# Second RWKV layer of a four-layer encoder: the first half of the key product by split parts, with a new table of rank offsets

## The chip, the cores and the metric

The kernel runs on one core of a Trainium2 chip. The metric is the device time of one execution in microseconds, as the median of several runs. TensorE (PE) multiplies matrices, VectorE (DVE) and ScalarE (ACT) work on tiles in the on-chip memory, GpSimd (POOL) does little here, and SyncE (SP) issues the DMAs.

## What is computed

Four layers with residual adds on an input of 256 tokens by 1024 channels in float32. Each layer is a token mixer and a SwiGLU FFN of 2816 inner channels, both behind an RMS norm. The mixers are, in order: RWKV-7 time mixing, stick-breaking attention, sparse attention over selected keys, and RWKV-7 again. The change is in the last of these. Of its reference only this bears on it:

```
shifted = jnp.pad(h, ((0, 0), (1, 0), (0, 0)))[:, :-1]
xm = h[:, :, None, :] + (shifted - h)[:, :, None, :] * mix
rkv = jnp.einsum('bsjd,jde->bsje', xm[:, :, :3], w_rkv)
r, k, v = rkv[:, :, 0], rkv[:, :, 1], rkv[:, :, 2]
...
kk = heads(k * k_k)
```

So the key `k` is a 1024 by 1024 product of the mixed input. From it, the decay and the gates come the factors of a recurrence over the tokens, which is computed in four chunks of 64 tokens for 16 heads.

## The kernel before

Activations lie with channels on the 128 partitions and the 256 tokens along the free axis, in eight channel blocks. Weights come from the DRAM in 401 pieces of 128 x 1024 float32 (`raw`, four buffers). There are two ways to multiply with such a piece:

- Unsplit: `raw_piece` hands the float32 piece to PE. PE's trace shows one such source matmul as two records.
- Split: `piece` copies the piece to the rounded type float32r (`wh`, a CAST, on ACT or DVE) and subtracts that from the piece on DVE (`wl`). The input is split in the same way (`split`: a cast for the high part, a subtraction on DVE for the low part). `mm3` then adds three products: `wh` by the high input, `wh` by the low input, `wl` by the high input. `wh` and `wl` have three buffers each.

`SPLITS` says for each of the two RWKV layers which products are split. A letter `k` splits the whole key product, and `K` its second half only. The key product has two halves of 512 output channels. The first half (key pieces `ka`, accumulated in two banks named `kp`) goes through the eight channel blocks in turn, as its inputs come from the norm; the second half (`gemm2`) follows from the stored split inputs `kx`. With `K`, the mixed input of a channel is written to `xk` in full, used there by the first half, and also split to `kx` for the second. With `k`, it is written to a small rotating tile `xm` and split to `kx`, which both halves use. The lines that choose:

```
sk, sk2, sv_ = [n in SPLITS[j] for n in "kKv"]
...
w = [v3(t, 2) for t in (piece(key) if sk else (raw_piece(key),))]
if sk:
    split(kx[:, 0, c], kx[:, 1, c], xm("mk", c))
else:
    mix(xk[:, c, :], "mk", c)
    if sk2:
        split(kx[:, 0, c], kx[:, 1, c], xk[:, c])
```

The order of the work around it: the FFN of the third layer ends with its down product (`dn`), whose last sum is added to `xt`. The squares (`sq`) are summed over the channels by PE (`ss`) and make the scale `rstd` (`rstdm`, `rstda`). DVE then forms the normed input and its difference to the previous token, both in `pre`, and the mixed inputs. PE meanwhile multiplies `lora_in`, which needs only `xt`. Behind the keys come the receptance `rp` (from `prx`), the gate `g`, the small products `lw` and `la` (64 rows of the array), `sc` (kept in `SB`), and the values `vp`. DVE copies 32x32 blocks of `SB` together (`blocks`), inverts them in 31 steps (`xtmp`, `inv`), copies the result to `XT` and transposes it (`xd`). The products `cmb` and then the recurrence (`xu`, `qu`, `pS`, `Y` on 64x64 parts of the array) follow, and the output product `po`.

The order within each engine isn't the order of the code. A planner (class `Plan`) records all operations, estimates a cost for each, ranks them by the longest path behind them, and schedules them by list over the engines. It chooses among engines where an operation can run on more than one (casts and copies on ACT or DVE), gives out the buffers, and puts in two filler matmuls at a time (`warm_o`) where PE would have too little to do in a stretch of time. It repeats this for 16 rounds, and then once more from its best with the table `NUDGES`: each entry (seed, first, last, width) draws random offsets for the ranks of a range of operations. The schedule with the shortest planned time is emitted.

Of the kernel before, what the change touches and what calls it, by code (L numbers as in the profile page):

```python
# [189 lines left out]
class Queue:  # L190
# [91 lines left out]

WAIT = {"tensor": 85.0, "vector": 55.0, "scalar": 40.0, "gpsimd": 40.0, "sync": 0.0}

SPLITS = ('K', 'K')
FREE = ("raw", "xm")

BIAS = {"vector": 2.0}
# [1753 lines left out]
```

## Time and profile before

| what | value |
|---|---|
| median of 3 runs | 1381.39 us (1380.25 to 1381.43) |
| the profiled execution's own time | 1380.69 us |
| its span, first to last instruction | 1378.9 us |
| fp32 `kp<-xk` matmul records, both RWKV layers | 128, of which 64 in the second |
| split `kp<-kx` matmul records, both layers | 192, of which 96 in the second |
| second RWKV layer, from the last down matmuls to the output product | about 1001 to 1190 us of the span |

Times in the profile are in microseconds from the span's start, means of one instruction in ns. A row of the timeline has start, length, engine, line, operation, out<-in, the shapes, and in brackets the idle time in front of it with what ended it. Rows with xN are N like instructions in a row; their lengths overlap, since an instruction's end is seen later than the next one's start. All operations have the line of the planner's call (L785), so the names of the tiles tell them apart.

### The profile page before, as it was taken

The page shows a single profiled execution, that of the slowest core. Times are in us where ns is not written, and L with a number is a line of the kernel's source. Part 1 is how long each engine was busy: PE and PEld are TensorE (multiplying, and loading weights), DVE is VectorE, ACT ScalarE, POOL GpSimd, SP SyncE. Part 2 cuts the span into 40 slices and gives each one's busy share as a digit, 9 for nine tenths or more (in the row PEclk, how much of TensorE's full clock was granted, in tenths as well). Part 3 has the DMA queues.
Part 4 walks back from the last instruction along what each step waited for, and adds up shares of the span by engine and source line. Part 5 has one row for each costly group of instructions (what it writes and reads, how often), then busy time and mean ns, then how long its engine had stood idle before and what let it go on. Part 6 is the DMA issues. An engine that isn't in the chain of part 4 may idle for free.

```text
span 1378.9 us, 25431 instructions
## 1 busy us (share of the span) xinstructions
PE 1368.9 (99%) x10134; PEld 1189.6 (86%) x10134; DVE 1123.5 (81%) x1981; ACT 765.2 (55%) x1285; POOL 7.5 (1%) x16
## 2 busy tenths in 40 slices
PE   9999999999999999999999999999999999999998
PEld 7988898888888898888887798888888888988887
DVE  7899688896676789886589888986589996899864
ACT  4866665454456755454456875444357466655432
POOL 0000000000000000000000000000000000000000
PEclk9999999999999999999999999999999999999999
DMA  5533155566654355555554445555534231556563
GB/s 188 171 106 109 39 177 184 183 198 188 198 169 154 108 153 190 193 185 193 189 183 154 160 133 189 189 194 187 195 93 141 93 95 47 169 187 195 185 209 112
DMA packets 61333, 220.04 MB, mean 160 GB/s; under 512 B 6816, under 2 KB 8352, under 8 KB 60960
## 3 DMA queue, kind: packets, MB, share of 16 engines
q1 hardware_dynamic: 61216, 218.44, 49.1%
q8 instruction: 79, 1.29, 0.4%
q14 instruction: 38, 0.31, 0.1%
HBM read 217.36 MB, written 1.05 MB: 158 GB/s over the span
## 4 chain that ended last, share of the span: by engine, by line
PE 94%; DVE 4%; ACT 1%; issue 0%; DMA 0%; SPq 0%; ACTq 0%; DVEq 0%
PE dn L785 18%; PE gate L785 18%; PE up L785 18%; PE po L785 7%; PE kp L785 4%; PE rp L785 3%; PE qk L785 3%; PE vps L785 3%; PE vp L785 2%; PE z L785 2%; PE q L785 2%; PE k L785 2%; PE sc L785 1%; PE lora_in L785 1%; PE Y L785 1%; PE attn_o L785 1%
## 5 line engine op out<-in xcount | busy, mean ns | idle before, releaser
L785 ACT CAST wh<-raw 128x1024 fp32r<-128x1024 f32 x339 | 354.7, 1051 | 356.5 <-PE dn L785 114.8
L785 DVE TENSOR_TENSOR wl<-raw,wh 128x1024 fp32r<-128x1024 f32 x375 | 453.2, 1220 | 75.9 <-ACT wh L785 69.6
L785 PE MATMUL up<-xg,wh 128*128 128x512 f32 x704 | 253.9, 395 | 0.0
L785 PE MATMUL gate<-xg,wh 128*128 128x512 f32 x704 | 253.4, 395 | 0.0
L785 PE MATMUL dn<-h,wh 128*128 128x512 f32 x720 | 247.3, 391 | 0.0
L785 PE MATMUL dn<-h,wl 128*128 128x256 f32 x704 | 197.3, 280 | 0.0
L785 PE MATMUL up<-xg,wl 128*128 128x256 f32 x704 | 196.9, 280 | 0.0
L785 PE MATMUL gate<-xg,wl 128*128 128x256 f32 x704 | 196.9, 280 | 0.0
L785 PEld LDWEIGHTS dn<-h,wh 128*128 128x128 f32 x720 | 134.2, 188 | 30.6
L785 PEld LDWEIGHTS gate<-xg,wh 128*128 128x128 f32 x704 | 132.0, 188 | 30.6
L785 PEld LDWEIGHTS up<-xg,wh 128*128 128x128 f32 x704 | 131.9, 187 | 30.5
L785 PEld LDWEIGHTS up<-xg,wl 128*128 128x128 f32 x704 | 132.9, 189 | 0.1
L785 PEld LDWEIGHTS gate<-xg,wl 128*128 128x128 f32 x704 | 132.9, 189 | 0.1
L785 PEld LDWEIGHTS dn<-h,wl 128*128 128x128 f32 x704 | 132.9, 189 | 0.0
L785 DVE TENSOR_TENSOR xt<-xt,dn 128x256 f32<-128x256 f32 x64 | 26.7, 418 | 42.4 <-PE dn L785 41.7
L785 DVE TENSOR_TENSOR gus<-gus,rstd 128x512 f32<-128x512 f32 x88 | 59.8, 685 | 1.1
L785 PE MATMUL vp<-xv,raw 128*128 128x256 f32 x256 | 57.7, 382 | 0.1
L785 PEld LDWEIGHTS vp<-xv,raw 128*128 128x128 f32 x256 | 47.8, 190 | 7.6 <-issue 0.7
L785 PE MATMUL rp<-prx,wh 128*128 128x256 f32 x256 | 50.1, 295 | 0.0
L785 PE MATMUL po<-yhl,wh 128*128 128x256 f32 x256 | 48.9, 291 | 0.1
L785 PE MATMUL po<-ohl,wh 128*128 128x256 f32 x256 | 48.3, 289 | 0.0
L785 PE MATMUL qk<-xg,wh 128*128 128x512 f32 x128 | 46.3, 403 | 0.0
(326 smaller groups left out, 2380.4 us busy)
## 6 DMA issues: line engine op xcount, KB each, us to landing
raw<-in_wts_dram SPq DMA_DIRECT2D x401, 512.0 KB, 3.6
lora<-in_lora_dram SPq DMA_DIRECT2D x2, 1280.0 KB, 9.6
xt<-in_xT_dram SPq DMA_DIRECT2D x4, 256.0 KB, 4.0
lora<-in_lora_dram SPq DMA_DIRECT2D x2, 512.0 KB, 5.3
inv<-in_id_dram SPq DMA_DIRECT2D x2, 512.0 KB, 4.6
out_dram<-xt SPq DMA_DIRECT2D x8, 128.0 KB, 1.9
sbt<-in_consts_dram SPq DMA_DIRECT2D x1, 512.0 KB, 4.2
consts<-in_consts_dram SPq DMA_DIRECT2D x1, 288.0 KB, 3.8
```

The costliest lines, as they stand in the source:

```text
L785: getattr(getattr(nc, o.eng), method)(*map(real, args), **{k: real(a) for k, a in kw.items()})
```

## The change

`SPLITS` gives the second RWKV layer `k` in place of `K`: its first half of the keys is multiplied by split parts of weights and inputs too, and `xk` falls away there. The first RWKV layer keeps `K`. The table `NUDGES` has other entries (219 for 221), which moves instructions in all layers.

```
-    (903826, 3056, 3356, 3000), (539854, 3023, 3143, 8000), (863608, 3279, 3287, 8000), (659967, 3402, 3452, 3000),
...
+    (258298, 3255, 3305, 300), (585931, 3338, 3458, 1000), (427633, 4293, 4593, 1000), (808878, 5009, 5029, 3000),
...
-SPLITS = ('K', 'K')
+SPLITS = ('K', 'k')
```

The whole program has 32 float32 key matmuls less (of the source), 96 split ones more, four casts to `wh` and four subtractions to `wl` more, and 12 filler matmuls more. Three places show how the order moves. The line of the planner's call is L784 in the changed kernel, since the table is a line shorter.

PE, from the end of the third layer's down product to the first key products of the second RWKV layer, before:

```order
L785 MATMUL dn<-h,wh_10335 128x256 x2
L785 MATMUL dn<-h,wl_10343 128x256
L785 MATMUL ss<-sq,ones 128x256
L785 MATMUL lora_in<-xt_69,lora 128x256 x4
L785 MATMUL ss<-sq,ones 128x256
L785 MATMUL lora_in<-xt_72,lora 128x256 x4
L785 MATMUL lora_in<-xt_73,lora 128x256 x4
L785 MATMUL lora_in<-xt_74,lora 128x256 x4
L785 MATMUL kp<-xk,raw_10282 128x256 x4
```

The same place in the changed kernel:

```order
L784 MATMUL dn<-h,wl_10343 128x256
L784 MATMUL ss<-sq,ones 128x256 x3
L784 MATMUL lora_in<-xt_69,lora 128x256 x2
L784 MATMUL ss<-sq,ones 128x256
L784 MATMUL lora_in<-xt_69,lora 128x256 x2
L784 MATMUL lora_in<-xt_72,lora 128x256 x4
L784 MATMUL lora_in<-xt_73,lora 128x256 x4
L784 MATMUL lora_in<-xt_74,lora 128x256 x4
L784 MATMUL kp<-kx,wh_10358 128x256 x2
L784 MATMUL kp<-kx,wl_10371 128x256
```

Two `ss` products that stood among the down products stand behind them now, and the first key products are split triples with the pieces 10358/10371.

DVE, from the last subtractions for the down product to the scale of the norm, before:

```order
L785 TENSOR_TENSOR wl_10320<-raw_10256,wh_10312 128x1024
L785 TENSOR_TENSOR wl_10343<-raw_10269,wh_10335 128x1024
L785 MEMSET pre 128x8
L785 TENSOR_TENSOR xt_74<-xt_74,dn 128x256 x4
L785 TENSOR_SCALAR rstdm<-ss 128x256
```

The same place in the changed kernel, where 10371, 10393 and 10421 are the first three key pieces:

```order
L784 TENSOR_TENSOR wl_10343<-raw_10261,wh_10333 128x1024
L784 TENSOR_TENSOR xt_74<-xt_74,dn 128x256 x2
L784 MEMSET pre 128x8
L784 TENSOR_TENSOR wl_10371<-raw_10285,wh_10358 128x1024
L784 TENSOR_TENSOR wl_10393<-raw_10321,wh_10385 128x1024
L784 TENSOR_TENSOR xt_74<-xt_74,dn 128x256 x2
L784 TENSOR_TENSOR wl_10421<-raw_10335,wh_10412 128x1024
L784 TENSOR_SCALAR rstdm<-ss 128x256
```

Two subtractions of key pieces stand between the adds of the last two channel blocks, and a third between the last adds and `rstdm`. The fourth key piece is subtracted later, among the key inputs:

```order
L784 SCALAR_TENSOR_TENSOR xm<-pre,vecs 128x256
L784 TENSOR_TENSOR wl_10551<-raw_10354,wh_10509 128x1024
L784 TENSOR_TENSOR kx<-xm,kx 128x256
L784 SCALAR_TENSOR_TENSOR pre<-xt_74,vecs,rstd 128x256
L784 TENSOR_TENSOR wl_10576<-raw_10381,wh_10547 128x1024
```

The first of these subtractions is for the key piece of channels 6 and 7; the second already belongs to the second half of the keys.

PE, ahead of the recurrence of the second RWKV layer, before (each filler has a row for its weights and one for its product):

```order
L785 MATMUL cmb_11863<-XT,zs 32x32 x16
L785 MATMUL xu<-QC,XT 64x64 x4
L1879 LDWEIGHTS warm_x
L1879 MATMUL warm_o<-warm_x 128x256
L1879 LDWEIGHTS warm_x
L1879 MATMUL warm_o<-warm_x 128x256
L785 MATMUL cmb_11893<-xd,SB 32x32 x16
```

and in the changed kernel:

```order
L784 MATMUL cmb_11899<-xd,SB 32x32 x16
L784 MATMUL bn<-prhl,bonesr 128x512 x2
L1878 LDWEIGHTS warm_x
L1878 MATMUL warm_o<-warm_x 128x256
L1878 LDWEIGHTS warm_x
L1878 MATMUL warm_o<-warm_x 128x256
L784 MATMUL cmb_11931<-XT,zs 32x32 x16
L1878 LDWEIGHTS warm_x
```

Before, gate products (`pg`) stood between the first `cmb` products and the fillers came behind the first `xu`, six of them up to the second `xu`; now the gate products are all ahead of `cmb`, and fourteen fillers stand between the first `cmb` and the second `xu`, the last row shown being the first of the next six.

109 rows, old and new, of the table NUDGES are left out of this document.

## Prediction

> **What bounds the kernel now.** I read the page first, then the windows over the second recurrent layer, then the timelines of TensorE (PE) and VectorE (DVE) in it.
>
> ```profile
> span 1378.9 us, 25431 instructions
> PE 1368.9 (99%) x10134; PEld 1189.6 (86%) x10134; DVE 1123.5 (81%) x1981; ACT 765.2 (55%) x1285; POOL 7.5 (1%) x16
> PE 94%; DVE 4%; ACT 1%; issue 0%; DMA 0%; SPq 0%; ACTq 0%; DVEq 0%
> ```
>
> PE is busy for all but 10 us and carries 94% of the chain that ended last. That is the mean of the whole kernel; the changed layer has to be read by itself. The windows (us; then busy time and count of PE, weight loads, DVE, ACT, POOL; PE clock; DMA) run from the last matmuls of the FFN before the layer to its output product:
>
> ```profile
> 1001.00:1011.00 10.00, 10.00 (x53) 8.94 (x53) 5.03 (x13) 3.81 (x7) 0.00 (x0) 1.00 0.01 2
> 1011.00:1048.00 37.00, 37.00 (x256) 33.75 (x255) 36.99 (x70) 28.06 (x53) 0.36 (x1) 1.00 0.50 157
> 1048.00:1063.00 15.00, 15.00 (x116) 12.80 (x115) 14.72 (x27) 12.66 (x24) 0.00 (x0) 1.00 0.43 120
> 1063.00:1083.00 20.00, 20.00 (x213) 17.87 (x211) 19.51 (x34) 8.90 (x16) 1.86 (x2) 1.00 0.24 76
> 1083.00:1100.00 17.00, 16.86 (x95) 13.73 (x96) 16.25 (x39) 5.66 (x12) 0.00 (x0) 1.00 0.35 113
> 1100.00:1137.00 37.00, 35.61 (x589) 30.52 (x587) 35.95 (x76) 25.12 (x48) 0.00 (x0) 1.00 0.28 92
> 1137.00:1175.00 38.00, 37.47 (x714) 31.23 (x711) 24.06 (x65) 23.91 (x65) 0.00 (x0) 1.00 0.15 48
> ```
>
> Here two engines are full at once. From 1011 to 1137 us DVE is busy for 95 to 100% of every window, as PE is; only behind 1137, in the recurrence proper, does DVE fall to 24.06 of 38 us. Which of the two is followed shows at the end of that stretch:
>
> ```profile
> 1129.33 1.28 PE L785 MATMUL cmb<-xd,SB 32*32 32x32 f32 x64 [0.73 <-DVE xd L785]
> 1136.12 0.61 PE L1879 MATMUL warm_o<-warm_x 128*128 128x256 bf16 x4
> 1138.15 0.25 DVE L785 TENSOR_SCALAR Sd<-Sn,dc 128x64 f32<-128x64 f32 x1 [0.52 <-ACT Sn L785]
> ```
>
> PE stood idle for 0.73 us until DVE had transposed the inverted blocks (`xd`); DVE's own first wait comes at 1138.15. So **DVE's work sets when the recurrence starts**, and PE is only just not late for it.
>
> **The change part by part.** The key product of the first half loses its unsplit form. One unsplit source matmul is two records of 128x256; a split one is three, two with `wh` and one with `wl`.
>
> ```profile
> 1010.74 10.52 PE L785 MATMUL kp<-xk,raw 128*128 128x256 f32 x48
> ...
> 1029.93 0.40 PE L785 MATMUL kp<-kx,wh 128*128 128x256 f32 x2
> 1030.17 0.28 PE L785 MATMUL kp<-kx,wl 128*128 128x256 f32 x1
> 1030.29 0.40 PE L785 MATMUL kp<-kx,wh 128*128 128x256 f32 x2
> ```
>
> 48 records in 10.52 us, the last of which lasts about 0.38, make (10.52 - 0.38)/47 = 0.216 us each, 0.432 a source matmul. A split triple repeats after 1030.29 - 1029.93 = 0.36 us, all three together. There are 32 (8 channels, 4 column blocks): 32 x (0.432 - 0.360) = **2.3 us less on PE**. [...] The row shows 0.360, so the sum uses that.
>
> What it costs: four weight pieces now need a cast (ACT) and a subtraction (DVE).
>
> ```profile
> L785 DVE TENSOR_TENSOR wl<-raw,wh 128x1024 fp32r<-128x1024 f32 x16 | 19.3, 1214 | 0.6 <-PE po L785 0.6
> L785 ACT CAST wh<-raw 128x1024 fp32r<-128x1024 f32 x12 | 12.5, 1042 | 2.5 <-DMA raw<-in_wts_dram 2.4
> ```
>
> Four casts are 4.2 us of ACT, busy 28.06 of 37 us in the tightest window; I cost them at nothing (bounds 0 and 1.0, one cast late). Four subtractions are 4.9 us of DVE, and here the order of the instructions decides. DVE before the layer:
>
> ```profile
> 999.93 0.42 DVE L785 TENSOR_TENSOR xt<-xt,dn 128x256 f32<-128x256 f32 x1
> 1003.17 0.88 DVE L785 TENSOR_TENSOR xt<-xt,dn 128x256 f32<-128x256 f32 x2 [2.82 <-PE dn L785]
> 1006.27 0.42 DVE L785 TENSOR_SCALAR rstdm<-ss 128x256 f32<-128x256 f32 x1 [2.22 <-ACT rstda L785]
> ...
> 1008.09 0.88 DVE L785 SCALAR_TENSOR_TENSOR pre<-xt,vecs,rstd 128x256 f32<-128x256 f32 x2
> 1008.88 0.76 DVE L785 TENSOR_TENSOR pre<-pre 128x256 f32<-128x256 f32 x2
> 1009.55 0.88 DVE L785 SCALAR_TENSOR_TENSOR xk<-pre,vecs 128x256 f32<-128x256 f32 x2
> ...
> 1013.00 0.42 DVE L785 TENSOR_TENSOR kx<-xk,kx 128x256 fp32r<-128x256 f32 x1
> ```
>
> There are two holes, 2.82 and 2.22 us. The new order puts two subtractions (2.4 us) in the first and one (1.2 us) in the second: three of four are covered. If the cover went (a cast late, a buffer still held by the down product), each would push the norm back by up to 1.2 us. The fourth stands between the key inputs of channel 6: 1.2 us exposed.
>
> *Start of the layer.* Two of the four `ss` products move behind the down product; each is two records of 128x256 like `xk`'s, 0.216 us, so it ends 0.9 us sooner. DVE is then still in its second subtraction, until 999.93 + 0.42 + 2 x 1.21 = 1002.8 against the add at 1003.17: the norm starts 0.4 us sooner (bounds 0 and -0.9).
>
> *Feeding PE.* From the starts above, a channel takes DVE 0.40 (`pre`) + 0.34 (shifted difference) + 0.40 (`xm`) + some 0.34 (`kx`) = 1.48 us, where PE now needs 4 x 0.36 = 1.44 (before, 8 x 0.216 = 1.73, with half the `kx` put off). So PE runs dry by about 0.1 us in some of the eight channels: +0.5 on PE (bounds 0 and 1.2).
>
> *DVE up to the last `xd`.* Counting the two orders from `rstdm` on: one `wl`, one `wh` cast, one `QC` and one `UV` copy and two short `gt` copies more; three `blocks` copies, a `prx` and a `prhl` cast and two `prs` scalings fewer.
>
> ```profile
> L785 DVE COPY blocks<-SB 32x512 f32<-32x512 f32 x5 | 3.5, 695 | 0.1
> L785 DVE CAST wh<-raw 128x1024 fp32r<-128x1024 f32 x4 | 2.6, 679 | 0.6 <-PE xu L785 0.6
> L785 DVE TENSOR_SCALAR prs<-pr,vecs 128x256 f32<-128x256 f32 x3 | 1.0, 340 | 0.0
> L785 DVE CAST prhl<-prs 128x512 fp32r<-128x512 f32 x2 | 0.8, 419 | 0.0
> L785 DVE CAST prx<-xr 128x512 fp32r<-128x512 f32 x2 | 0.8, 414 | 0.0
> ...
> L785 ACT COPY QC<-qct 128x512 f32<-128x512 f32 x8 | 4.4, 582 | 0.1
> L785 ACT COPY blocks<-SB 32x512 f32<-32x512 f32 x3 | 3.3, 1107 | 8.3 <-DVE SB L785 8.3
> ```
>
> The `QC` and `UV` copies are not on DVE before; I take ACT's 0.58 for each, 1.16 for both. 1.21 + 0.68 + 1.16 - 3 x 0.70 - 0.41 - 0.42 - 2 x 0.34 = -0.6 us; the `gt` copies take some of it back: I take -0.5 (bounds -0.9, and +1.2 if the `blocks` copies, 1.1 us each on ACT, hold up the inversion and only the `wl` counts). With the start: **the recurrence begins 0.9 us sooner** (bounds -1.8 and +1.2). Where do PE's 2.3 us go? Into waiting for `xd`: the new order holds 14 filler matmuls between the `cmb` products and the second `xu`, where 6 stood.
>
> *The recurrence.* Over the kernel there are 12 fillers and 8 changes between whole-array and part-array matmuls more. Four fillers in 0.61 us, the last about 0.28 long, are 0.11 each: 1.3 us. The price of leaving part of the array:
>
> ```profile
> 1022.82 0.38 PE L785 MATMUL la<-tl,lora 64*128 64x256 f32 x1
> 1023.12 0.50 PE L785 MATMUL kp<-kx,wh 128*128 128x256 f32 x2
> 1023.46 0.28 PE L785 MATMUL kp<-kx,wl 128*128 128x256 f32 x1
> ```
>
> From `la` to the `wl` behind it are 0.64 us, of which 0.216 + 0.24 are work: 0.18 a change, 1.5 us for eight. Both may lie in time in which PE waits anyway (0) or on the path (2.8). On the other side DVE has two `wh` casts fewer in this stage, 2 x 0.68 = 1.4, on an engine busy 24 of 38 us. I take -0.4 for all (bounds -1.4 and +2.8). The other layers are reordered without a change of work; the table moves them by 0, give or take 1.
>
> Sum: -0.9 - 0.4 = **-1.3 us**. The profiled execution took 1380.69 us (span 1378.9), which gives 1379.4; the median of the runs is 0.7 above it, at 1381.39, so the forecast for a median is **1380.1 us**. About 0.2%, 2.8 us, is what a measurement can tell from no change.
>
> **The rivals.**
>
> 1. *PE was the path after all.* For it: PE 94% of the chain, 37.00 of 37. Then its 2.3 us come out whole beside DVE's 0.9: 1381.39 - 3.2 = 1378.2, and 1376.8 with the -1.4 of the recurrence. Against it: DVE as full, and the 0.73 us wait for `xd`. Chance 0.32.
>
> 2. *DVE is the path into the recurrence and PE inside it.* Place: between the last `xd` and the output product. The fourth subtraction is exposed (+1.2), and the fillers and changes of the array come on the path (+2.8): 1381.39 + 4.0 = 1385.4. It decides if `xd` comes no sooner after the down product than before and PE has no idle time in 1137 to 1175; PE's 37.47 of 38 us speak for it, but a filler is issued where the plan has nothing else ready. Chance 0.15.
>
> 3. *The clock falls.* PE gets emptier, and the windows show a granted clock of 1.00 with the old fill. If the 37 us up to 1137 ran at 0.9, they would be 4 us longer: 1384.1 with the forecast's other terms. Longest idle time here 0.73 us, and fillers are added: chance 0.03. [...]
>
> That the change doesn't do what it says is out: the new order has 32 `kp<-xk` matmuls fewer and 96 `kp<-kx` more, all of the difference in the second layer.
>
> **How the numbers follow.** Forecast 0.50 (1378.8 to 1382.6), rival 1 0.32, rival 2 0.15, rival 3 0.03. Rival 1 ends below 1378.6 in nearly all its cases, rivals 2 and 3 mostly above 1384.2, the lower prices of rival 2 within. Faster 0.32, same 0.52, slower 0.16. The range cuts off the outer part of rivals 1 and 2, one tenth each: 1377.0 to 1384.4.
>
> **What would show it.** `kp<-xk` falls from 128 records to 64 and the triples keep 0.36 us. DVE's two holes before `rstdm` are filled. The first `xd` comes 0.9 us sooner after the last down matmul; if by 2 or more, rival 1. PE's idle time and fillers ahead of the recurrence grow by about 2 us. The recurrence, from the first `xu` to the output product, keeps its length; if it grows by over 2 us, rival 2. A clock under 1.00 would be rival 3. A subtraction behind `rstdm`, or a first-layer stage moved by over 1 us, would make the sum wrong.

## The result and the profile after

| what | before | changed |
|---|---|---|
| median | 1381.39 us (1380.25 to 1382.87, 5 runs) | 1389.34 us (1386.79 to 1393.49, 5 runs) |
| ratio | | 1.006, 95% interval 1.0049 to 1.0071 |
| the profiled execution's own time, and span | 1380.69, 1378.9 us | 1387.45, 1385.6 us |

The changed kernel is slower by 0.6%, some 8 us, outside the range that was given. The page of the changed kernel, the three lines that answer to the first ones shown above:

```profile
span 1385.6 us, 25531 instructions
PE 1373.0 (99%) x10178; PEld 1191.6 (86%) x10178; DVE 1127.0 (81%) x1983; ACT 772.7 (56%) x1291; POOL 11.5 (1%) x16
PE 89%; DVE 8%; DMA 1%; issue 1%; ACT 0%; SPq 0%; DVEq 0%; ACTq 0%
```

PE is as busy in share, but busy for 4.1 us more (1373.0 against 1368.9), although it has less to multiply, and DVE's share of the chain that ended last has doubled. Where the time went is found by putting the same events of the two traces side by side (us from the span's start):

| event | before | changed | later by |
|---|---|---|---|
| first `gate` matmul of the first FFN | 191.0 | 193.1 | 2.1 |
| first `gate` of the second FFN | 493.9 | 495.8 | 1.9 |
| first `gate` of the third FFN | 817.3 | 820.5 | 3.2 |
| last `dn` of the third FFN (the changed layer begins) | 1002.9 | 1007.3 | 4.4 |
| first `xd` of the changed layer | 1128.5 | 1132.4 | 3.9 |
| first `gate` of the fourth FFN (the changed layer ends) | 1189.9 | 1194.8 | 4.9 |
| last `dn` of the fourth FFN | 1374.7 | 1381.4 | 6.7 |

Of 6.7 us, **4.4 are lost before the changed layer begins and 1.8 behind it**. The layer itself, in which the split was made, takes 187.5 us for 187.0 (all of this in the two profiled executions).

The 4.4 and the 1.8 have one cause in common, for a part of each, which the rows of the wide `gate` matmuls show when each FFN is asked for by itself. A row has the least, the median and the largest length in ns, then the starts of the first and the last. Before, first to fourth FFN:

```profile
L785 PE MATMUL gate<-xg,wh x176: 387/391/404, 191.0 to 309.4; 128*128 128x512 f32 x176
L785 PE MATMUL gate<-xg,wh x176: 395/398/583, 493.9 to 613.1; 128*128 128x512 f32 x176
L785 PE MATMUL gate<-xg,wh x176: 391/391/403, 817.3 to 934.7; 128*128 128x512 f32 x176
L785 PE MATMUL gate<-xg,wh x176: 391/395/579, 1189.9 to 1307.3; 128*128 128x512 f32 x176
```

and the changed kernel:

```profile
L784 PE MATMUL gate<-xg,wh x176: 392/395/403, 193.1 to 310.8; 128*128 128x512 f32 x176
L784 PE MATMUL gate<-xg,wh x176: 395/398/403, 495.8 to 615.0; 128*128 128x512 f32 x176
L784 PE MATMUL gate<-xg,wh x176: 395/398/403, 820.5 to 939.7; 128*128 128x512 f32 x176
L784 PE MATMUL gate<-xg,wh x176: 395/398/403, 1194.8 to 1314.0; 128*128 128x512 f32 x176
```

The work in the four is the same, and the profile shows no wait of PE in it, but it runs at one of two speeds. Read to the ns in the records, a pair (one matmul of 128x512, one of 128x256) repeats on average either every 346.7 ns or every 353.3 ns. At 346.7 all pairs are alike (230 ns from the wide matmul to the narrow one), or two kinds alternate (231 and 233 ns). At 353.3 there is a cycle of three pairs, in which those distances are 241, 236 and 233 ns; below, a pair is called by this number. Each FFN begins at 353.3. Before, the third and the fourth FFN ran at 346.7 from their 840th and 1208th us on (117.4 us from first to last `gate`); in the changed kernel neither does (119.2). That is 1.8 us each, 3.6 of the 6.7.

A second cause is in the spread. The mean granted clock of the five executions was 1.000 twice (1386.79 and 1387.45 us), 0.998 twice (1389.34 and 1390.64) and 0.995 once (1393.49). The profiled one is among the quick ones, so its trace doesn't show this loss; the median lies 1.9 to 2.6 us above the two at 1.000.

### The profile page after: what moved, and what is told of

Its sections match the earlier page's. It is cut to its first block, busy times and chain, and to the rows that moved or that the text cites. A ratio compares the mean times of both kernels' runs of the same rounds, so it can differ in the third digit from the quotient of the medians.

```text
span 1385.6 us, 25531 instructions
## 1 busy us (share of the span) xinstructions
PE 1373.0 (99%) x10178; PEld 1191.6 (86%) x10178; DVE 1127.0 (81%) x1983; ACT 772.7 (56%) x1291; POOL 11.5 (1%) x16
## 3 DMA queue, kind: packets, MB, share of 16 engines
HBM read 217.36 MB, written 1.05 MB: 158 GB/s over the span
## 4 chain that ended last, share of the span: by engine, by line
PE 89%; DVE 8%; DMA 1%; issue 1%; ACT 0%; SPq 0%; DVEq 0%; ACTq 0%
PE gate L784 18%; PE up L784 18%; PE dn L784 17%; PE po L784 7%; PE kp L784 3%; PE vps L784 3%; PE rp L784 3%; PE qk L784 3%; PE z L784 2%; DVE inv L784 2%; PE k L784 2%; PE q L784 2%; DVE xtmp L784 1%; PE Y L784 1%; DVE SB L784 1%; PE attn_o L784 1%
## 5 line engine op out<-in xcount | busy, mean ns | idle before, releaser
L784 ACT CAST wh<-raw 128x1024 fp32r<-128x1024 f32 x343 | 359.5, 1051 | 360.7 <-PE dn L784 112.4
L784 DVE TENSOR_TENSOR wl<-raw,wh 128x1024 fp32r<-128x1024 f32 x379 | 458.4, 1220 | 80.0 <-ACT wh L784 71.8
L784 PE MATMUL up<-xg,wh 128*128 128x512 f32 x704 | 256.5, 399 | 0.0
L784 PE MATMUL gate<-xg,wh 128*128 128x512 f32 x704 | 255.1, 398 | 0.0
L784 PE MATMUL dn<-h,wh 128*128 128x512 f32 x720 | 247.2, 390 | 0.0
L784 PE MATMUL dn<-h,wl 128*128 128x256 f32 x704 | 197.3, 280 | 0.0
L784 PE MATMUL up<-xg,wl 128*128 128x256 f32 x704 | 197.2, 280 | 0.0
L784 PE MATMUL gate<-xg,wl 128*128 128x256 f32 x704 | 197.2, 280 | 0.0
L784 PEld LDWEIGHTS dn<-h,wh 128*128 128x128 f32 x720 | 134.1, 188 | 30.7
L784 PEld LDWEIGHTS gate<-xg,wh 128*128 128x128 f32 x704 | 132.2, 188 | 32.4
L784 PEld LDWEIGHTS up<-xg,wh 128*128 128x128 f32 x704 | 132.2, 188 | 32.3
L784 PEld LDWEIGHTS up<-xg,wl 128*128 128x128 f32 x704 | 132.8, 189 | 0.2
L784 PEld LDWEIGHTS dn<-h,wl 128*128 128x128 f32 x704 | 133.0, 189 | 0.0
L784 PEld LDWEIGHTS gate<-xg,wl 128*128 128x128 f32 x704 | 132.9, 189 | 0.0
L784 DVE TENSOR_TENSOR gus<-gus,rstd 128x512 f32<-128x512 f32 x88 | 59.9, 685 | 0.9
L784 PE MATMUL vp<-xv,raw 128*128 128x256 f32 x256 | 57.7, 382 | 0.0
L784 PEld LDWEIGHTS vp<-xv,raw 128*128 128x128 f32 x256 | 47.8, 190 | 7.5 <-issue 0.6
L784 DVE TENSOR_TENSOR xt<-xt,dn 128x256 f32<-128x256 f32 x64 | 26.8, 418 | 30.7 <-PE dn L784 29.9
L784 PE MATMUL rp<-prx,wh 128*128 128x256 f32 x256 | 50.7, 298 | 0.0
L784 PE MATMUL po<-yhl,wh 128*128 128x256 f32 x256 | 48.8, 291 | 0.4 <-DVE xt L784 0.4
L784 PE MATMUL po<-ohl,wh 128*128 128x256 f32 x256 | 48.1, 288 | 0.0
L784 PE MATMUL qk<-xg,wh 128*128 128x512 f32 x128 | 46.3, 402 | 0.5 <-DVE xg L784 0.5
```

What stands on the lines that cost most here:

```text
L784: getattr(getattr(nc, o.eng), method)(*map(real, args), **{k: real(a) for k, a in kw.items()})
```

## The experiments

### Which part of the program loses

The texts written ahead of the runs call the explanations by letters. A: the new order of the other layers costs the time; B: the split itself does; C: the falls of the clock; D and P: the place of the `ss` products sets the speed of the FFN.

Four kernels ran on one chip, on which the kernel before took 1381.14 us. The first is the changed kernel again.

> The changed kernel once more, nothing altered, to see how far its runs lie apart on another chip and which granted clock they show. Theory A (the order that the new table gives to the other layers is the cause): again +5 to +10 us over the kernel before, ratio 1.004 to 1.007. Theory C (the clock falls in some executions: 0.995 to 0.998 in three of the five runs so far, 1386.8 to 1393.5 us): runs at clock 1.000 lie within 1 us of 1387, runs at 0.998 some 2 to 3 us above, at 0.995 some 6 above.

Measured: 1386.88 us, ratio 1.0045 (1.0033 to 1.0057). The loss is there again, though smaller: 5.7 us. Three of these five executions ran at a clock of 1.000, so this median holds none of the clock's loss.

The second and the fourth keep the new split and put the old entries of the table back where they steer the first three layers (first operation below 4922); the fourth has no entries at all for the last layer:

```
 NUDGES = [[
-    (258298, 3255, 3305, 300), (585931, 3338, 3458, 1000), (427633, 4293, 4593, 1000),
+    (903826, 3056, 3356, 3000), (539854, 3023, 3143, 8000), (863608, 3279, 3287, 8000),
...
 SPLITS = ('K', 'k')
```

> SPLITS as changed; the table has the old entries for the operations of the first three layers (index under 4922) and the new ones behind. The order of all engines up to the last RWKV layer is then word for word that of the kernel before; only the last RWKV layer and its FFN differ. Theory A (the split is about neutral, the new order of the first three layers costs): the third layer's down product ends at 1002.9 us of the span as before (within 0.5), the last RWKV layer takes 187 us (within 2), the whole within 0.2% of before. Theory B (the split itself costs): the last RWKV layer takes 190 or more, the whole is 5 us or more over before.

> As e1, but the table has no entries behind the third layer: the split key product in a third order of the last layer. Theory A: up to 1002.9 us as before; the last RWKV layer within 3 us of 187, depending on the order alone. Theory B: 190 or more, as in e1. Theory D: the last FFN's pitch is 346.7 or 353.3 ns whatever the time of the RWKV layer, 2 us between the two.

The third is the reverse: the old split, the new entries for the first three layers, the old ones for the last (`SPLITS = ('K', 'K')`).

> SPLITS as before ('K', 'K'); the table has the new entries for the first three layers and the old ones behind, so the order up to the last RWKV layer is word for word that of the changed kernel, and no product is split otherwise. Theory A: the third layer's down product ends at 1007.3 us of the span as in the changed kernel (within 0.5, so 4.4 later than before), the whole is 4 to 6 us over before. Theory B: within 0.2% of before. Theory D (the pitch of the FFN's matmul pairs, 346.7 or 353.3 ns, is set by where the ss products stand in it): the third FFN stays at 353.3 ns here, as in the changed kernel, and goes over to 346.7 in e1.

Measured, for the second, the fourth and the third: 1389.52 us (1.0061, 1.0049 to 1.0073), 1387.34 (1.0046, 1.0034 to 1.0058) and 1390.3 (1.0065, 1.0049 to 1.008). By their totals all three are as slow as the changed kernel, which theory A had not expected of any of them; the second and the fourth look like theory B (190 us or more in the last layer), and the third, without the split, speaks against B. The traces separate the causes. With the old order in front, the third FFN ends as in the kernel before, with the new one it ends late, whatever the split. The last `dn` of the second, fourth and third of these kernels:

```profile
L956 PE MATMUL dn<-h,wl x176: 277/280/284, 940.9 to 1002.9; 128*128 128x256 f32 x176
```

```profile
L773 PE MATMUL dn<-h,wl x176: 277/280/284, 941.0 to 1003.0; 128*128 128x256 f32 x176
```

```profile
L783 PE MATMUL dn<-h,wl x176: 277/280/284, 944.2 to 1006.6; 128*128 128x256 f32 x176
```

So the 4.4 us belong to the order of the first three layers. What the three lost instead, they lost in the last layer: 195.4, 191.1 and 196.9 us from there to the next `gate`, where the kernel before and the changed one take 187.0 and 187.5. (The 196.9 hold 13.65 us at half the clock, from 1140.9 us on; executions of that kernel at a clock of 1.000 took 6 us less than the profiled one.) A table entry fits the plan that it was searched with; beside another front or split it makes a poor order, so these totals can't price the split.

Two more kernels settle that. One is the twin of the fourth, but with the old split. The other puts two orders together as they are: the planner's results are written out as a fixed list, the first three layers from the kernel before, the last from the changed kernel.

> The old split ('K', 'K') with the order of the kernel before in the first three layers and no table entries for the last layer: the twin of the run before it with the new split ('K', 'k') and no entries for the last layer (1387.34 us; its RWKV layer took 191.1 us from the last down product to the first gate product, where 187.0 are the kernel before's). Theory A (the split itself is worth nothing either way, and the 4 us in that twin's RWKV layer come from a poorer order of the last layer): this one is as poor, 1386 to 1389 us, RWKV layer 190 to 192 us. Theory B (splitting the first half of the keys costs about 4 us by itself): RWKV layer 187 us and 1381.5 to 1384 us. The pitch of the last FFN (353.3 or 346.7 ns a pair) can shift either total by 1.8 us and is read apart from the trace.

> The two orders put together: the first three layers in the order of the kernel before, instruction by instruction, and the last layer (with the new split) in the order of the changed kernel. Theory A (the changed kernel lost 4.4 us by the new order of the first three layers, 0.5 in the RWKV layer with the split, and 1.8 in the last FFN by the 353.3 ns pitch): the last down product of the third layer ends at 1003, the RWKV layer takes 187 to 188 us, the last FFN 186.6 at 353.3 ns or 184.8 at 346.7: 1383.4 us (1381.6 at the fast pitch). Theory B (the loss sits in the split layer or follows from it): 1386 us or more, with an RWKV layer above 190 us.

Measured: the twin 1387.2 us (1.0046, 1.0034 to 1.0058) against 1387.34; its RWKV layer took 191.3 us, in which its profiled execution ran for 3.41 us at half the clock, which can have cost it up to 1.7 (half of 3.41, an estimate). The composed kernel took 1385.28 us (1.0032, 1.0019 to 1.0045), but 1382.89 to 1383.16 in its three executions at a clock of 1.000, where 1383.4 had been expected. **The split costs or brings no 4 us; the order of the first three layers costs them.**

### The two speeds of the FFN

In the traces the speed of the `gate` and `up` pairs changes where the `ss` products (fp32, two records each) interrupt them (the one other change in 18 profiles stands behind a pause of 0.06 us, in the changed kernel with moved products and fillers, at 305 us), so their place was varied, and nothing else. In these kernels the planner's result stands as a fixed list in which the rows of PE shown are moved; a few weight buffers change places with that. First, the changed kernel with the products of three FFNs moved later, by one, two and one pairs, each behind a 241; and the kernel before with three groups moved away from the 241. The edit of the second kernel in the first FFN:

```
 MATMUL up<-xg,wl 128x256
-MATMUL ss<-sqa,ones 128x256 x2
 MATMUL up<-xg,wh 128x512
 MATMUL up<-xg,wl 128x256
+MATMUL ss<-sqa,ones 128x256 x2
 MATMUL up<-xg,wh 128x512
```

> The changed kernel, word for word the same order on all engines but for the ss products of the second, third and fourth FFN, which stand one, two and one gate/up pairs later on PE (six matmuls in all). Theory P: in the gate and up stream a pair of matmuls repeats every 353.3 ns in a cycle of three (the wide matmul 241, 236, 233 ns) or every 346.7 ns, and the ss products decide which: behind a pair with the 241 they lead to 346.7, behind one with 236, and as a pair behind 233, they stay at 353.3. All three are moved behind a 241. Then the second, third and fourth FFN run at 346.7 from there on: -1.9, -2.0 and -1.9 us, together -5.8, and 1381 to 1383.5 us against the 1386.9 and 1389.3 of the changed kernel. Rival (the pitch is given by something else, such as the buffers' places or the weights' transfers, and only accompanies the ss products): the pitches stay at 353.3, the total within 1 us of the changed kernel's, or up to 1 us above it because the scale of the norm comes up to 0.7 us later.

> The kernel before, the same order on all engines but for the ss products of the first, third and fourth FFN: those of the first stand one pair later, the second product of the third and of the fourth directly behind the first, and the fourth's one pair later, so that each group stands behind a pair with the 236. Theory P (the place of the ss products in the cycle of three pairs sets the pitch): the three FFNs that ran at 346.7 ns a pair stay at 353.3, 1.8 to 2.0 us each: 1386.4 to 1387.2 us against 1381.1. Rival (the pitch is given by something else): the pitches stay at 346.7 and the time within 0.7 us of 1381.1.

Measured for the second: 1385.91 us (1.0038, 1.0026 to 1.0051), 5.3 above the 1380.58 of the kernel before on that chip, 1.8 for each FFN; 1386.4 or more had been expected, so the way was right and the size a little less. It multiplies what the kernel before multiplies. The wide `up` matmuls of the third FFN from 845 to 930 us, grouped, in the kernel before, in this one, and in the changed kernel (count, then busy us and mean ns):

```profile
L785 PE MATMUL up<-xg,wh 128*128 128x512 f32 x128 | 45.8, 391 | 0.0
```

```profile
L857 PE MATMUL up<-xg,wh 128*128 128x512 f32 x120 | 43.8, 399 | 0.0
```

```profile
L784 PE MATMUL up<-xg,wh 128*128 128x512 f32 x122 | 44.4, 399 | 0.0
```

In this FFN the second of the two products had been moved two pairs ahead, from behind a 241 to the first one, behind a 236; that turned 391 into 399, as in the changed kernel. The reverse held less cleanly, and its total missed the 1381 to 1383.5 us that had been expected: the changed kernel with moved products took 1380.59 us in its profiled execution, with all three FFNs at 346.7 and a clock of 1.000, but 1386.89 in the median of eight, at clocks of 0.995 to 0.999. And in its third FFN, where the products had been moved by two pairs, PE paused for 0.2 us one or two pairs ahead of them without a wait that the profile shows.

Two kernels tried the same on the kernel before, whose second FFN never ran at 346.7, again by two pairs, the second with 12 fillers at PE's start, where PE of the kernel before is busy for 1.57 us from 8 to 10 us and for 1.22 us from 10 to 12:

> The kernel before with one edit: the ss products of the second FFN, the one that stays at 353.3 ns a pair there, stand two pairs later, behind a pair with the 241 ns. Theory P: the pitch is 346.7 from there on, -1.8 to -1.9 us, 1378.7 us against 1380.6 (ratio 0.9987). Rival (the second FFN is slow for another reason): within 0.4 us of the kernel before.

> The run above with 6 fillers ahead of the first ss and 6 ahead of the first lora_in. Theory C: the executions at a clock of 0.999, which cost 1.5 us each and are a third of those of the kernel before, get rarer, since the thin stretch at 9 to 12 us is fuller; the median stays at 1378.7 to 1379.2, and the highest of the runs falls from about 2 us above the median to under 1. Rival: the fillers delay lora_in by up to 0.6 us and the spread stays, 1379.3 us.

Measured: 1380.13 us (0.9995, 0.9987 to 1.0004) and 1381.02 (1.0, 0.9991 to 1.0009). Both missed: the second FFN stayed at 353.3 ns, with a pause of 0.2 us just ahead of the products. What the fillers did can't be told apart from that.

So the move was made by one pair in the other direction, in the second FFN of the kernel before and in the third of the changed kernel:

> The kernel before with one edit on PE: the two ss products of the second FFN stand one pair earlier, behind the pair with the 241 ns instead of the one with the 236. Theory P: from there on 346.7 ns a pair instead of 353.3, 99 us of the FFN, -1.9 us: 1379.2 us against 1381.1 (ratio 0.9986). Rival (the second FFN is slow for another reason): 353.3 ns and within 0.4 us of the kernel before.

> The changed kernel with the ss products of the second FFN one pair later, of the third one pair earlier, of the fourth one pair later, all behind a 241. Theory P: all three run at 346.7 ns in every execution, -5.8 us at equal clock: 1380.6 to 1381.5 us where the clock is 1.000. Where it is lower, each 0.001 of the mean clock stands for 1.4 us at half speed and costs up to as much, so with clocks of 0.995 to 0.998 as before the median comes out at 1382 to 1386. Rival to P: 353.3 ns in the third FFN as in the run with fillers, 1382.6 at a clock of 1.000.

The first took **1378.21 us, ratio 0.9982 (0.9974 to 0.9991)**: the second FFN runs at 346.7, and the kernel is faster than the kernel before and the changed one. PE's timeline of the kernel before around the products (start, length):

```profile
509.06 0.40 PE L785 MATMUL up<-xg,wh 128*128 128x512 f32 x1
509.30 0.28 PE L785 MATMUL up<-xg,wl 128*128 128x256 f32 x1
509.42 0.40 PE L785 MATMUL up<-xg,wh 128*128 128x512 f32 x1
509.66 0.28 PE L785 MATMUL up<-xg,wl 128*128 128x256 f32 x1
509.77 1.03 PE L785 MATMUL ss<-sqa,ones 128*128 128x256 f32 x4
510.45 0.58 PE L785 MATMUL gate<-xg,wh 128*128 128x512 f32 x1
```

and of the one with the products one pair earlier:

```profile
509.15 0.40 PE L857 MATMUL up<-xg,wh 128*128 128x512 f32 x1
509.39 0.28 PE L857 MATMUL up<-xg,wl 128*128 128x256 f32 x1
509.51 1.02 PE L857 MATMUL ss<-sqa,ones 128*128 128x256 f32 x4
510.19 0.59 PE L857 MATMUL up<-xg,wh 128*128 128x512 f32 x1
...
511.07 0.39 PE L857 MATMUL up<-xg,wh 128*128 128x512 f32 x1
511.31 0.28 PE L857 MATMUL up<-xg,wl 128*128 128x256 f32 x1
511.42 0.39 PE L857 MATMUL up<-xg,wh 128*128 128x512 f32 x1
511.65 0.28 PE L857 MATMUL up<-xg,wl 128*128 128x256 f32 x1
511.77 0.39 PE L857 MATMUL gate<-xg,wh 128*128 128x512 f32 x1
```

From there the length of the wide matmul reads 0.39, and 511.77 - 511.07 is 0.70 for two pairs, where the slow cycle has 0.71. The second kernel's three FFNs ran at 346.7 as well, and its three executions at a clock of 1.000 took 1380.20 to 1380.27, where the changed kernel at that clock took 1385.80 to 1387.45; the others, at 0.993 to 0.996, made its median 1384.55 (1.0022, 1.0011 to 1.0033).

Over all 18 profiles of this study, many of which share stretches of the order: both `ss` products in a row directly behind a 241, with no pause ahead of them, led to 346.7 in 18 of 18 places; behind a 236 to 353.3 in 12 of 12; behind a 233 to 353.3 in 3 of 3. With a pause ahead of them it was 353.3 in four of five. This holds for two products in a row. A single one behind a 233 led to 346.7 as well, in the first FFN of the changed kernel and of the six others with its order there, and two products one pair apart in its fourth FFN, the first behind a 233, left it at 353.3.

### The clock

In the changed kernel PE, with 2.3 us less work in the keys, has no gate products left when it comes to the first `cmb` products, small ones of 32x32, and waits for their inputs (`xd`; in the profiled execution `gT`, a copy on ACT, came last). The rows, where the one of the kernel before (shown in the prediction) has a wait of 0.73 and gate products behind it:

```profile
1132.50 0.28 PE L784 MATMUL pg<-gy,wy 96*128 96x256 f32 x1
1133.83 1.20 PE L784 MATMUL cmb<-xd,SB 32*32 32x32 f32 x64 [1.05 <-ACT gT L784]
```

No profile of the changed kernel shows a fall of the clock there; the one fall that a profile of it caught is at PE's start, 3.41 us at half the clock from 12.53 us on. In kernels with the same order of the last layer but other `ss` places the wait is 1.57 or 1.58 us, and there falls were caught: 3.41 us from 1131.88 on in the composed kernel (a clock of 0.50 in the window from 1132 to 1134 us; it fell at 12.3 us as well), and a longer one, shown below. Not every execution falls: one with a wait of 1.58 us kept its clock.

Fillers in that wait, and at PE's start, were tried with the `ss` products moved by two pairs, in the whole changed kernel and in the composed one. Theory C, with the falls in these two places, put the first at 1380.6 to 1383 us and at a clock of 0.998 or more in nearly all runs:

> The changed kernel with the three groups of ss products moved behind a pair with the 241 ns (as in the run before of that kind, 1380.59 us at a clock of 1.000, but 1386.89 in the median of 8 at 0.995 to 0.999), and with fillers in three places where PE waits: 6 matmuls ahead of the first ss, 6 ahead of the first lora_in, and 12 (1.3 us) in the wait of 1.6 us for the first xd of the last layer, ahead of its cmb products. [...] Rival (the falls come in the recurrence at 1135 to 1155, or are set by something else than PE's fill at these places): the median stays at 1385 to 1388 and the clock at 0.995 to 0.997.

> The first three layers in the order of the kernel before, the last (new split) in the order of the changed kernel, the ss products of the second FFN two pairs and of the fourth one pair later (behind a 241), and the same fillers. The same without the ss moves and fillers took 1382.9 to 1383.2 us at a clock of 1.000 and 1385.28 in the median. Theories P and C together: -1.9 for the second FFN, -1.9 for the fourth, clock 0.998 or more: 1379.0 to 1380.5 us, below the kernel before (1380.6 on that chip). If the split layer holds a loss of its own, or the fillers push the recurrence back by their 1.3 us: 1381 us or more.

Measured: 1385.12 us (1.0034, 1.0021 to 1.0046) and 1381.43 (1.0002, 0.9993 to 1.0011). Both totals are above what was expected. In each one FFN stayed at 353.3, with the pause of 0.2 us, so the totals mix two things; the clocks rose (from 0.995 to 1.000 without fillers to 0.997 to 1.000, and from 0.993 to 1.000 to 0.999 to 1.000). The profile of the first still fell, for 3.41 us at 685.85, in another layer. The clean pair is the kernel with products moved by one, above, and the same with 12 fillers in the `xd` wait alone:

```
 MATMUL pg<-gy,wy 96x256
+MATMUL warm_o<-warm_x 128x256 x12
 MATMUL cmb<-xd,SB 32x32 x16
```

> The run above with 12 filler matmuls more, in the 1.6 us that PE waits for the first xd of the last layer, ahead of its cmb products. Theory C (most of the clock's falls begin in this stretch): the mean clock of the executions rises by 0.002 or more against the run above, and the median falls by 2 to 4 us, to 1380.6 to 1382.5. Rival (the falls begin elsewhere: PE's start, the start of the third layer, the recurrence itself): clock and median as in the run above, within 1 us.

Measured: **1380.64 us (1.0, 0.9991 to 1.0008), 3.9 us below its twin**, the mean of its clocks 0.9995 against 0.9965. The profiled execution of the twin caught a fall. Its PE rows, and windows of 4 us (busy time and count of PE, weight loads, DVE, ACT, POOL; clock; DMA):

```profile
1125.48 0.28 PE L858 MATMUL pg<-gy,wy 96*128 96x256 f32 x1
1127.33 1.64 PE L858 MATMUL cmb<-xd,SB 32*32 32x32 f32 x64 [1.57 <-DVE xd L858]
1128.90 1.22 PE L858 MATMUL bn<-prhl,bonesr 128*128 128x512 f32 x2
```

```profile
1121.00:1125.00 4.00, 4.00 (x55) 3.60 (x53) 3.94 (x7) 3.40 (x6) 0.00 (x0) 1.00 0.05 18
1125.00:1129.00 4.00, 2.43 (x72) 2.19 (x70) 3.93 (x8) 2.85 (x6) 0.00 (x0) 0.85 0.02 4
1129.00:1133.00 4.00, 4.00 (x46) 2.35 (x48) 3.97 (x6) 2.52 (x5) 0.00 (x0) 0.50 0.00 0
1133.00:1137.00 4.00, 4.00 (x62) 3.05 (x64) 1.38 (x2) 1.56 (x5) 0.00 (x0) 0.50 0.55 209
```

The clock goes to half behind the wait of 1.57 us, in the products that set the start of the recurrence, and stays there for 10.24 us by the record of the clock. That takes 0.004 off this execution's mean clock, so 0.001 stands for some 2.8 us at half speed, twice what the text ahead of this twin has. With the fillers:

```profile
1126.67 1.48 PE L1952 MATMUL warm_o<-warm_x 128*128 128x256 bf16 x12
1128.39 1.20 PE L858 MATMUL cmb<-xd,SB 32*32 32x32 f32 x64 [0.23 <-DVE xd L858]
```

```profile
1125.00:1129.00 4.00, 3.77 (x67) 3.36 (x67) 3.94 (x8) 3.22 (x6) 0.00 (x0) 1.00 0.00 0
1129.00:1133.00 4.00, 4.00 (x120) 3.07 (x115) 3.92 (x7) 3.70 (x9) 0.00 (x0) 1.00 0.03 8
```

The fillers lie inside the wait (0.23 us of it is left), and the first `cmb` product starts 126.6 us behind the last `dn` in both, so they cost nothing themselves. The effect of the clock shows behind it: from the first `xd` to the next FFN's first `gate` it is 66.6 us in the twin's profile and 62.5 with the fillers.

### The split with its own order of the last layer

With the speed of the FFNs and the clock out of the way, the last kernel is the 1378.21 one with the changed last layer in place of the old:

> First three layers in the order of the kernel before, with the ss products of the second FFN one pair earlier; the last layer (new split) in the order of the changed kernel with the ss products of its FFN one pair later and the 12 fillers ahead of cmb. Twin of the first run of this set with the split in place. Theory A (the split itself is worth nothing either way): 1379.2 us, within 0.8 us of that run. If the split were worth the 0.9 us that was forecast for the start of the recurrence and no more: 1378.3. If it costs: 1380.5 or more.

Measured: 1379.44 us, ratio 0.9991 (0.9983 to 1.0), 1.2 us above its twin, more than the 0.8 that was allowed. In the traces the layer takes 187.2 us for 186.1. The composed kernel with fillers, whose second FFN ran at 353.3 as in the kernel before, gives 1.0002. The two intervals overlap, so the totals alone don't establish a cost of 1.2 us; a gain of 1.3, as forecast, is not to be seen.

The other traces speak for the cost. Seven profiles with the last layer in the changed kernel's order and no fall of the clock in it take 187.2 to 187.7 us there. Of five profiles with the old one in the order of the kernel before, four take 186.0 to 186.1; the first one, the kernel before's, takes 187.0. So the changed layer, split and order together, is about 1 us longer, not shorter. No run separates the two: the last layer's order changes with the split.

## Why the prediction was wrong, point by point

1. *PE saves 2.3 us in the keys.* Right. Of the 128 `kp<-xk` records 64 are left, and the triple kept its 0.36 us, from the first product on:

```profile
1016.46 0.40 PE L784 MATMUL kp<-kx,wh 128*128 128x256 f32 x2
1016.69 0.28 PE L784 MATMUL kp<-kx,wl 128*128 128x256 f32 x1
1016.81 0.40 PE L784 MATMUL kp<-kx,wh 128*128 128x256 f32 x2
```

2. *Three of four subtractions hide in DVE's two holes, and the norm starts 0.4 us sooner.* The place was right, the 0.4 was not:

```profile
1002.97 1.23 DVE L784 TENSOR_TENSOR wl<-raw,wh 128x1024 fp32r<-128x1024 f32 x1 [0.16 <-ACT wh L784]
1005.82 1.23 DVE L784 TENSOR_TENSOR wl<-raw,wh 128x1024 fp32r<-128x1024 f32 x1 [1.62 <-ACT wh L784]
1007.67 0.88 DVE L784 TENSOR_TENSOR xt<-xt,dn 128x256 f32<-128x256 f32 x2 [0.62 <-PE dn L784]
1008.67 1.22 DVE L784 TENSOR_TENSOR wl<-raw,wh 128x1024 fp32r<-128x1024 f32 x1
1010.76 0.43 DVE L784 TENSOR_SCALAR rstdm<-ss 128x256 f32<-128x256 f32 x1 [0.87 <-ACT rstda L784]
```

The holes of 2.82 and 2.22 us are filled, with 1.62 us of waiting for a cast in the first. `rstdm` comes 1010.76 - 1007.3 = 3.5 us behind the last `dn`, before 1006.27 - 1002.9 = 3.4: the norm starts no sooner.

3. *PE runs dry by 0.5 us in feeding.* It did not: the waits of PE show none from 1000 to 1062 us.

4. *The recurrence begins 0.9 us sooner.* The first `xd` comes 125.1 us behind the last `dn`, before 125.6: 0.5, within the bounds. That is partly luck, since the reason given, that DVE's work sets this start, doesn't fit the kernel before. DVE is nearly full there, but its rows show waits ahead of the one at 1138.15 (0.2 us at 1059.09, 0.4 at 1065.08), and the chain that ended last runs through PE up to 1119.0 us, then through copies on ACT up to 1126.2, and through DVE only for the rest of the way to `cmb`. In the changed kernel it runs through PE up to 1081.9 and through DVE (`SB`, `inv`, `xtmp`) from there to 1128.9, then through ACT. PE's saving shortened the path that led, and DVE's, almost as long, took over. The pages show it in the chain's shares by line, before and after:

```profile
PE dn L785 18%; PE gate L785 18%; PE up L785 18%; PE po L785 7%; PE kp L785 4%; PE rp L785 3%; PE qk L785 3%; PE vps L785 3%; PE vp L785 2%; PE z L785 2%; PE q L785 2%; PE k L785 2%; PE sc L785 1%; PE lora_in L785 1%; PE Y L785 1%; PE attn_o L785 1%
```

```profile
PE gate L784 18%; PE up L784 18%; PE dn L784 17%; PE po L784 7%; PE kp L784 3%; PE vps L784 3%; PE rp L784 3%; PE qk L784 3%; PE z L784 2%; DVE inv L784 2%; PE k L784 2%; PE q L784 2%; DVE xtmp L784 1%; PE Y L784 1%; DVE SB L784 1%; PE attn_o L784 1%
```

5. *The recurrence gains 0.4 (bounds -1.4 and +2.8).* From the first `xd` to the next FFN it is 62.4 us for 61.4, 1.0 more. It repeats: 62.4 to 62.5 in the seven profiles named above, against 60.8 in four and 61.4 in one with the old last layer. Rival 2 named the place of this loss, though not its condition, since `xd` did come sooner; which of the fillers, the changes of the array or other moves make it was not tried. Points 2 to 5 together make +0.5 where -1.3 stood; the bounds held it.

6. **"The other layers are reordered without a change of work; the table moves them by 0, give or take 1." This is the step that failed**, by 6.2 us: +4.4 in front of the layer and +1.8 behind it in the profiled execution. It took equal work for equal time. Of the 6.2, 3.6 are the two FFNs whose pairs stay at 353.3 ns because their `ss` products came to stand elsewhere in the cycle; the runs that move nothing else showed that both ways (+5.3 us with three FFNs; -2.7 with one, of which 1.9 lie in that FFN). The rest, 2.6 net, was not taken apart by runs; 2.1 of it came before the first FFN, in the first RWKV layer, whose work is the same. The prediction had named this as a sign that its sum would be wrong (a first-layer stage moved by over 1 us). It isn't all the order's: in six profiles with the new order there and no fall of the clock, the first `gate` comes at 191.4 to 193.1 us, in ten with the old order at 190.7 to 191.5. What is longer in all of them is the way from the first `xd` to that `gate`, 61.5 to 62.5 us against 60.0 to 60.5: PE in the ten us around its `xd` wait, before and after,

```profile
130.00:140.00 10.00, 9.88 (x236) 8.06 (x235) 9.71 (x17) 7.45 (x18) 0.00 (x0) 1.00 0.01 3
```

```profile
130.00:140.00 10.00, 8.80 (x237) 7.39 (x238) 9.34 (x16) 6.37 (x15) 0.00 (x0) 1.00 0.01 3
```

   is idle for 1.1 us more. The two speeds stood in the trace of before (391 and 398 ns in the rows of its FFNs); a reader of them would have given this term bounds of -1.8 (the second FFN gained) and +5.4 (three lost), not 1.

7. *Rival 3, the clock falls* (chance 0.03). It came: it is the 1.9 to 2.6 us by which the median of the first five executions lies above those at a clock of 1.000 (in the second five the median has none of it). For its place there is evidence from kernels with the same last layer: PE got emptier where it waits for `xd`, and fillers there took 3.9 us off. In the changed kernel itself the only fall that a profile caught is at PE's start, so how its own falls divide between the two places stays open. The argument against this rival, that the longest idle time was 0.73 us, looked at the order of before; in the new one the wait is 1.05 us in the profiled execution of the changed kernel and 1.57 in the kernel whose fall is shown above. The prediction's own sentence, that PE's saving would go "into waiting for `xd`", had this wait in hand.

The forecast was 9.2 us too low: by 6.2 for point 6, by 1.8 for points 2 to 5 (+0.5 in place of -1.3), and by 1.2 for the way from the profiled execution to the median, 1.9 us in place of the 0.7 of the kernel before, which is the clock's.

## What to carry to other kernels

When an edit brings a new order, the stages that it doesn't mean to change are a term of their own: read in the trace of before how fast they run at best and at worst for the same work, and give the term those bounds. PE time saved ahead of a wait is to be followed into the wait: here the one ahead of the first `cmb` products was 0.73 us before, 1.05 in the changed kernel and 1.57 in the one with products moved by one pair. In a profiled execution of the last the clock was at half for 10.24 us behind that wait; 12 fillers inside the wait took 3.9 us off the median, and the first `cmb` product started 126.6 us behind the last `dn` with and without them. To price one part of such a change, freeze the order of the rest instruction by instruction, since a searched table doesn't carry over.

## What was not expected of the hardware

- In the FFNs of these kernels a stream of the same pairs of matmuls had two lasting pitches (times from pair to pair), 346.7 and 353.3 ns, and which of them came went with where the four short records of two `ss` products interrupt the cycle of three: directly behind a 241, with no pause ahead of them, it was 346.7 in 18 of 18 places, behind a 236 353.3 in 12 of 12. What holds the slower cycle in place was not found. Nor was the cause of the pause of 0.2 us that came in all five profiles in which products were moved two pairs later; it didn't come where one was moved two pairs ahead.
- The falls of the clock inside a program that the 18 profiles caught lasted 3.41 us, or three or four times that. There are seven: 3.41 us at 12.53 in the changed kernel, at 12.3 and 1131.88 in the composed one, at 1100.96 and 685.85 in two others, 10.24 in the run above, 13.65 in the third kernel of the first set. Two of these kernels have the old split. Executions of the same program differ: over ten of the changed kernel the mean clock lay between 0.995 and 1.000. Ahead of the fall of 10.24 us the longest wait of PE was 1.57 us, with 32x32 products behind it. What starts a fall and what sets its length was not shown.
